# A hybrid decoder layer in split precision: low parts and square sums one step behind, four operand buffers in the down stages, and square sums by matmul

## Chip, core and metric

The kernel runs on one core of a Trainium2 chip. The metric is the device time of one execution in microseconds (us); the median of three executions is compared. TensorE (PE in the views) multiplies, VectorE (DVE) and ScalarE (ACT) do the element work, GpSimd (POOL) a little of it, and SyncE (SP) and GpSimd issue the DMAs.

## What is computed

One decoder layer on 1024 tokens of width 1024, in float32: a gated feed-forward network, a mixing block (windowed attention beside an mLSTM, their gated sum through an output matrix), a second network, and a final norm.

```
x = x + 1/2 * SwiGLU_1(RMSNorm(x))
h = RMSNorm(x); z = h @ W_in + b_in
...
x = x + (sigmoid(g_attn) * y_attn + sigmoid(g_mlstm) * y_mlstm) @ W_out
x = x + 1/2 * SwiGLU_2(RMSNorm(x))
final: RMSNorm(x).
...
def rms_norm(x, g):
    xf = x.astype(jnp.float32)
    y = xf * lax.rsqrt(jnp.mean(xf * xf, axis=-1, keepdims=True) + NORM_EPS)
    return (y * g.astype(jnp.float32)).astype(x.dtype)

def swiglu(x, w_gate, w_up, w_down):
    return (jax.nn.silu(x @ w_gate) * (x @ w_up)) @ w_down
```

## The kernel before

**Two parts of a number.** A float32 operand is split into a high part that TensorE takes (ScalarE copies and rounds it) and a low part, the difference (DVE subtracts). A product is three matmuls: high by high, high by low, low by high. The function `parted` issues copy and subtraction one behind the other, so that the subtraction is next on DVE when the copy has just gone to ScalarE. Weights (buffers `whi`, `wlo`, four of each) and activations are split in this way.

**Seven products instead of eight.** In both networks the operands are cut in halves in both directions, and seven products of sums replace eight. They have numbers; `PRODUCTS` gives the order 1, 2, 6, 7, 5, 4, 3. The tokens are cut into two halves of 512, h = 0 and 1. Sums of the weights' quarters are made on DVE by `sum_of`.

**The first stage of a network (`gate_up`)** goes through 11 steps s, in each through seven products p, for each of gate and up (w), with 12 matmuls of 128 x 512 each (L421); a few steps at the beginning take the products in a different order, since the activations for products 6, 7, 5, 4 and 3 come from the generator `lead`, which the code advances between the products. Weights are split by `split` ahead of their use, and the evacuations (L429 to L469) end in the combination of the seven products. Its results are written to a buffer `gd` in HBM.

**The second stage (`ffn`)**, called the down stage here, walks over three chunks c of the inner dimension (4, 4 and 3 tiles: `DOWN`) and seven products p; a step (c, p) takes its moving operand from `gd` with one DMA (`fetch`, L571, 2 MB or 1.5 MB, issued by GpSimd) into one of two buffers, and does four groups dp of 12 or 9 matmuls times the chunk's tiles (L632). The chunk's weights (`load`, from `dn`, four DMAs on SyncE) go to two buffers by turns. In the last chunk the outputs are complete and `done` is called for each of them: it takes their squares for the next norm.

**Norms.** `stats` squares one 128 x 512 tile on ScalarE (L253) and adds it to a running sum on DVE (L255). `rstd_rows` sums over partitions by four small matmuls (L262), adds the epsilon on DVE and takes the power on GpSimd (L264). `spread` brings the result to all partitions by four transposes (L270) and a copy on ScalarE (L272).

**The order** is written by hand: within a function by the order of the calls, across stages by generators. `pump()` advances those in the list `bg` (norm of the next stage, constants) by one yield each; `prepare()` issues the next weight's split. All engines run their own instructions in the order in which they are issued, and wait for each other by semaphores.

**Seams between stages**, by their place in the profile: the start (0 to 34 us), first network's first stage (to 458 us) and down stage (to 680 us), mixing of the two halves (L316 to L318 are its large products; the boundary of the halves is at 1205 us), the output product of the second half (L1481 adds the residual, L1449 is the first multiplication of the second network's norm for the first half), second network's first stage (from 1770 us) and down stage (from 2225 us), and the final norm at the end.

## Time and profile before

| what | value |
| --- | --- |
| median of 3 runs | 2463.17 us (2459.67 to 2466.4) |
| profiled execution, its own time | 2461.28 us |
| span in the profile | 2459.5 us |
| TensorE busy | 2357.0 us (96% of the span) |
| DVE busy | 1741.3 us (71%) |
| ScalarE busy | 940.8 us (38%) |
| GpSimd busy | 259.6 us (11%) |
| mean granted clock of TensorE | 0.980 |

The profiled execution lasts 1.8 us longer than its span, which begins with the first instruction. The granted clock is 1.00 at full speed and 0.50 at half; a mean over a stretch between them says how much of it ran at half. Busy time of TensorE contains matmuls that run slower at half clock, so 96% does not mean that only 4% is lost.

### The profile page before, as it was taken

What the parts mean: (1) busy time and instruction counts of PE and PEld (TensorE: products, weight loads), DVE (VectorE), ACT (ScalarE), POOL (GpSimd) and SP (SyncE); (2) the same over time, 40 slices, a digit from 0 to 9 for tenths busy, and PEclk for the clock granted to TensorE, in tenths of its full rate; (3) what the DMA queues carried; (4) which work ended last, traced back from release to release, by engine and by line L of the source; (5) the groups of instructions that cost most, each with busy time, mean ns of one, the idle gap of its engine ahead of it and who ended that gap; (6) DMA issues with size and microseconds to landing.
All of it is one profiled execution on the core that took longest, in us unless ns stands there. A gap on an engine that the chain in (4) does not pass through costs nothing.

```text
span 2459.5 us, 30117 instructions
## 1 busy us (share of the span) xinstructions
PE 2357.0 (96%) x11094; PEld 1951.4 (79%) x11094; DVE 1741.3 (71%) x2780; ACT 940.8 (38%) x1664; POOL 259.6 (11%) x246
## 2 busy tenths in 40 slices
PE   8899999989988999999999999999999999999995
PEld 7788888778877878888777878888778888887885
DVE  6989888856768864555568854545579987887666
ACT  5334334312236642333346632333343433332223
POOL 0000000000045320000134410000000000000001
PEclk8999999999999999999999999999999999999997
DMA  5355443995621213222541222222535544569653
GB/s 187 103 192 179 156 154 129 345 343 176 226 90 61 67 61 99 69 83 83 161 123 48 61 71 88 80 80 86 191 117 168 191 156 146 169 232 364 228 191 126
DMA packets 154324, 361.46 MB, mean 147 GB/s; under 512 B 13504, under 2 KB 22848, under 8 KB 154176
## 3 DMA queue, kind: packets, MB, share of 16 engines
q1 hardware_dynamic: 131728, 277.79, 34.5%
q0 software_dynamic: 21584, 81.53, 9.8%
q8 instruction: 88, 1.44, 0.2%
q14 instruction: 60, 0.49, 0.1%
q10 hardware_dynamic: 864, 0.21, 0.0%
HBM read 263.27 MB, written 96.21 MB: 146 GB/s over the span
## 4 chain that ended last, share of the span: by engine, by line
PE 58%; DVE 16%; issue 16%; DMA 5%; ACT 3%; POOL 1%; SPq 0%; DVEq 0%; POOLq 0%; ACTq 0%
PE mm L421 15%; PE mm L632 11%; PE mm L316 8%; PE mm L318 7%; PE mm L317 7%; DMA s<-gd 3%; DVE P L1048 1%; PE mm L909 1%; DVE PT L1087 1%; PE mm L910 1%; PE mm L911 1%; DMA gd<-nsq 1%; DVE wlo L336 1%; DVE P L1068 1%; DVE wlo L87 1%
## 5 line engine op out<-in xcount | busy, mean ns | idle before, releaser
L421 PE MATMUL mm<-s,whi 128*128 128x512 f32 x2112 | 657.4, 392 | 13.5 <-ACT nsq L460 8.7
L421 PEld LDWEIGHTS mm<-s,whi 128*128 128x128 f32 x2112 | 399.3, 189 | 99.9 <-ACT nsq L460 9.5
L316 PE MATMUL mm<-s,whi 128*128 128x512 f32 x1056 | 424.4, 402 | 1.0 <-ACT whi L75 1.0
L318 PE MATMUL mm<-s,wlo 128*128 128x512 f32 x1056 | 416.6, 394 | 6.2 <-DVE wlo L87 4.7
L317 PE MATMUL mm<-s,whi 128*128 128x512 f32 x1056 | 414.9, 393 | 0.0
L421 PE MATMUL mm<-s,wlo 128*128 128x512 f32 x1056 | 413.7, 392 | 0.0
L632 PE MATMUL mm<-s,whi 128*128 128x512 f32 (+1 forms) x1256 | 388.2, 391 | 14.0 <-DMA s<-gd 12.8
L632 PEld LDWEIGHTS mm<-s,whi 128*128 128x128 f32 x1256 | 237.7, 192 | 65.0 <-issue 10.3
L632 PE MATMUL mm<-s,wlo 128*128 128x512 f32 (+1 forms) x628 | 244.7, 390 | 0.0
L318 PEld LDWEIGHTS mm<-s,wlo 128*128 128x128 f32 x1056 | 200.2, 190 | 52.5 <-DVE wlo L87 6.0
L316 PEld LDWEIGHTS mm<-s,whi 128*128 128x128 f32 x1056 | 200.7, 190 | 42.7 <-issue 2.8
L421 PEld LDWEIGHTS mm<-s,wlo 128*128 128x128 f32 x1056 | 200.0, 189 | 41.6
L317 PEld LDWEIGHTS mm<-s,whi 128*128 128x128 f32 x1056 | 200.8, 190 | 38.1
L87 DVE TENSOR_TENSOR wlo<-wraw,whi 128x1024 fp32r<-128x1024 f32 (+1 forms) x138 | 169.6, 1229 | 67.2 <-ACT whi L75 66.6
L75 ACT ACTIVATE whi<-wraw 128x1024 fp32r<-128x1024 f32 (+1 forms) x154 | 159.7, 1042 | 68.1 <-DMA wraw<-wpa 20.6
L335 ACT ACTIVATE whi<-wr 128x1024 fp32r<-128x1024 f32 (+1 forms) x122 | 127.8, 1048 | 129.7 <-PE mm L421 83.3
L336 DVE TENSOR_TENSOR wlo<-wr,whi 128x1024 fp32r<-128x1024 f32 (+1 forms) x122 | 147.8, 1212 | 36.6 <-ACT whi L335 36.6
L335 ACT ACTIVATE whi<-s 128x1024 fp32r<-128x1024 f32 (+1 forms) x72 | 71.1, 987 | 250.9 <-PE mm L632 239.0
L571 POOL DMA_DIRECT2D s<-gd x42 | 31.8, 756 | 1165.6 <-PE mm L421 404.8
L632 PEld LDWEIGHTS mm<-s,wlo 128*128 128x128 f32 x628 | 120.2, 191 | 24.2
L336 DVE TENSOR_TENSOR nsq<-nsq 128x512 fp32r<-128x512 f32 x162 | 110.4, 685 | 24.4 <-ACT nsq L335 23.9
L429 ACT ACTIVATE nsq<-nsq 128x512 f32<-128x512 f32 x66 | 41.8, 633 | 216.6 <-DVE nsq L469 205.2
(274 smaller groups left out, 3519.5 us busy)
## 6 DMA issues: line engine op xcount, KB each, us to landing
gd<-nsq SPq DMA_DIRECT2D x308, 256.0 KB, 3.1
s<-gd POOLq DMA_DIRECT2D x28, 2048.0 KB, 10.6
wraw<-win SPq DMA_DIRECT2D x84, 512.0 KB, 3.6
wr<-gu SPq DMA_DIRECT2D x74, 512.0 KB, 4.7
s<-gd POOLq DMA_DIRECT2D x14, 1536.0 KB, 6.7
s<-dn SPq DMA_DIRECT2D x16, 1024.0 KB, 12.4
wraw<-gu SPq DMA_DIRECT2D x30, 512.0 KB, 4.8
nsq<-x SPq DMA_DIRECT2D x32, 256.0 KB, 6.8
```

Source lines behind the costliest of these rows:

```text
L75: self.nc.scalar.activation(hv, v, AF.Copy)
L87: (self.nc.gpsimd if self.on_pool else self.nc.vector).tensor_sub(lv, v, hv.bitcast(F32))
L316: nc.tensor.matmul(ps, hi, xh, start=first, stop=False)
L317: nc.tensor.matmul(ps, hi, xl, start=False, stop=False)
L318: nc.tensor.matmul(ps, lo, xh, start=False, stop=last)
L335: nc.scalar.activation(hi, x, AF.Copy)
L336: nc.vector.tensor_sub(lo, x, hi.bitcast(F32))
L421: nc.tensor.matmul(ps, a[:, k], op[p](k, x), start=first and k == 0 and j == 0, stop=k == 3 and j == 2, skip_group_check=not first)
L429: nc.scalar.activation(t, z[0], AF.Tanh, scale=0.5)
L571: nc.gpsimd.dma_start(t, gd[PRODUCTS.index(p), s0:s0 + a].rearrange("s p i t -> p s i t"))
L632: nc.tensor.matmul(ps, wt[:, f], t[:, f, x, c], start=first and f == 0 and q == 0, stop=f == a - 1 and q == 2, skip_group_check=not first)
L909: nc.tensor.matmul(ps, x[:, 0], hi, start=k == 0, stop=False)
```

## The change

- `parted` no longer issues the subtraction: it returns a function, and the caller calls it later. In the weights' splits (`gate_up`, `ffn`) the high part is issued in the first half of a product's work and the low part in the second, just ahead of the sums and loads that stood there; in the operands of a norm (`mixed`, `early`) and in the products' combination (L460 to L469) the low part comes one tile behind its high part.
- `stats` holds its addition back until the next square has been issued; `flush` issues what is left ahead of the sum over partitions.
- In the start, the second half's squares are no longer added up on DVE: `mean_square` sums each over partitions on TensorE, all eight into one PSUM tile. 16 matmuls on an identity matrix (`warm`) follow, and only then the first product.
- The down stages take the products in the order 1, 2, 6, 7, 4, 5, 3. They have four buffers for the moving operand, and a fetch is issued three steps ahead. The weights of all chunks share one place of four quarters, and the next chunk's quarters are loaded as soon as their place has been read.
- Two small ones: the tile `nv` of a norm has two buffers, and at the boundary of the halves the norm waits for eight pumps instead of three.

```diff
+DOWN_ORDER = (1, 2, 6, 7, 4, 5, 3)
...
     def stats(pool, acc, x, first, eng=nc.vector):
+
         sq = pool.tile([128, HS], F32, name="nsq", bufs=nbufs(pool))[:, :x.shape[-1]]
         nc.scalar.activation(acc if first else sq, x, AF.Square)
+        flush()
         if not first:
-            eng.tensor_add(acc, acc, sq)
...
+            held.append(lambda: eng.tensor_add(acc, acc, sq))
...
+    def mean_square(ps, sq, k):
+
+        for b in range(4):
+            nc.tensor.matmul(ps[:, b], sq[:, 128 * b:128 * b + 128], mean, start=k == 0 and b == 0,
+                             stop=k == KT - 1 and b == 3, skip_group_check=True)
...
     def parted(x, hi, lo):
         nc.scalar.activation(hi, x, AF.Copy)
-        nc.vector.tensor_sub(lo, x, hi.bitcast(F32))
+        return lambda: nc.vector.tensor_sub(lo, x, hi.bitcast(F32))
...
                 part = [temp(pool, R32) for _ in range(2)]
-                parted(x, *part)
+                lo = parted(x, *part)
+                yield
+                lo()
                 for i in range(2):
                     nc.sync.dma_start(gd[PRODUCTS.index(p), s, :, i], part[i].bitcast(F32))
-                yield
                 if sub:
                     sub[0](*sub[1:])
-                    yield
...
-            split(*nxt)
+            lo = split(*nxt)
+            yield
+            lo()
             done += 1
...
-        steps = [(c, p) for c in range(len(DOWN)) for p in PRODUCTS]
+        steps = [(c, p) for c in range(len(DOWN)) for p in DOWN_ORDER]
...
-            if b == 0:
-                raw[c] = slot((0, 2, 0)[c], [16 * HS], F32)
-            m, h = divmod(b, 2)
-            t = raw[c][:, b * 4 * a * 128:][:, :4 * a * 128]
+            if c == m == h == 0:
+                raw["all"] = slot(0, [4, 4 * HS], F32)
+            place = {(0, 0): 0, (0, 1): 3 if c == 1 else 1, (1, 0): 2, (1, 1): 1 if c == 1 else 3}[m, h]
+            t = raw["all"][:, place, :4 * a * 128]
...
-                t = moving["buf"][:, i % 2, :a]
+                b = (i + 1) % 4
+                t = moving["buf", b // 2][:, b % 2, :a]
...
+            yield
+            low()
+            if p in (1, 2, 6, 7):
+                sum_of(c, j, {1: 3, 2: 2, 6: 1, 7: 4}[p])
+            if j and c + 1 < len(DOWN) and p in (7, 4, 5, 3):
+                load(c + 1, *{7: (0, 0), 4: (0, 1), 5: (1, 0), 3: (1, 1)}[p])
+            yield
...
             elif p == 7:
-                moving["buf"] = slot(1, [2, 4, 2, HS])
+                moving["buf", 0] = slot(1, [2, 4, 2, HS])
                 fetch(0)
-                fetch(1)
...
+            elif p == 4:
+                moving["buf", 1] = slot(2, [2, 4, 2, HS])
+                for i in range(1, 4):
+                    fetch(i)
...
             if i:
-                fetch(i + 1)
+                fetch(i + 3)
...
-            if 1 <= i % 7 <= 4 and c < last:
-                load(c + 1, i % 7 - 1)
...
+        ps1 = psum.tile([128, 4, 2], F32, name="mm")
+
+        def square1(k):
+            sq = temp(pool)
+            nc.scalar.activation(sq, X[k][1], AF.Square)
+            mean_square(ps1, sq, k)
+
+        for k in range(5):
+            square1(k)
         for r in rs:
             pass
+        for k in range(5, KT):
+            square1(k)
+        warm(16)
...
-        bg.append(norm(op, psum, lambda k: xb[:, k], 1, Hcur))
+        bg.append(norm(op, psum, lambda k: xb[:, k], 1, Hcur, wait=8))
...
         for k in range(KT):
             nc.vector.scalar_tensor_tensor(X[k][0], X[k][0], gains[:, 2, k:k + 1], r, op0=OP.mult, op1=OP.mult)
-            parted(X[k][0], t0[:, k, 0], t0[:, k, 1])
-            yield
+            nxt = parted(X[k][0], t0[:, k, 0], t0[:, k, 1])
+            if lo:
+                lo()
+            lo = nxt
```

How this moves instructions is seen in the programs' order at three places. Line numbers are each kernel's own. First TensorE at the start, of the kernel before: matmuls on the identity, the first half's mean sums (L262), their spread (L270) and the first product (L421).

```order
L691 MATMUL mm<-ident 128x128 x36
L262 MATMUL mm<-mean,nsq 128x2 x4
L270 MATMUL mm<-ident,nv 128x128 x4
L421 MATMUL mm<-s_135,whi 128x512 x2
L421 MATMUL mm<-s_135,wlo 128x512
```

The same place after the change: L273 and L281 are the sums and the spread of the first half, L289 the second half's sums, L735 the warming matmuls, L443 the first product.

```order
L718 MATMUL mm<-ident 128x128 x36
L273 MATMUL mm<-mean,nsq 128x2 x4
L289 MATMUL mm<-mean,nsq 128x2 x20
L281 MATMUL mm<-ident,nv 128x128 x4
L289 MATMUL mm<-mean,nsq 128x2 x12
L735 MATMUL mm<-ident 128x128 x16
L443 MATMUL mm<-s_135,whi 128x512 x2
L443 MATMUL mm<-s_135,wlo 128x512
```

Five of the eight sets of sums have come ahead of the spread, three sets and 16 matmuls between it and the first product.

Second, DVE during the output product before the second network, before the change: L87 is a low part of the weights, L1481 the residual, L1449 the multiplication of the norm and L336 the low part of its result, L255 the addition of a square.

```order
L87 TENSOR_TENSOR wlo<-wraw,whi 128x1024
L1481 SCALAR_TENSOR_TENSOR nsq<-mm,nsq 128x512
L1449 SCALAR_TENSOR_TENSOR nsq<-nsq,gains 128x512
L336 TENSOR_TENSOR s_13653<-nsq,s_13653 128x512
L1449 SCALAR_TENSOR_TENSOR nsq<-nsq,gains 128x512
L336 TENSOR_TENSOR s_13653<-nsq,s_13653 128x512
L87 TENSOR_TENSOR wlo<-wraw,whi 128x1024
L1449 SCALAR_TENSOR_TENSOR nsq<-nsq,gains 128x512
L336 TENSOR_TENSOR s_13653<-nsq,s_13653 128x512
L1481 SCALAR_TENSOR_TENSOR nsq<-mm,nsq 128x512
L255 TENSOR_TENSOR nsq<-nsq 128x512
```

And after it (L88, L1529, L1491, L353 and L264 in that order):

```order
L1529 SCALAR_TENSOR_TENSOR nsq<-mm,nsq 128x512
L1491 SCALAR_TENSOR_TENSOR nsq<-nsq,gains 128x512 x2
L353 TENSOR_TENSOR s_13689<-nsq,s_13689 128x512
L88 TENSOR_TENSOR wlo<-wraw,whi 128x1024
L1529 SCALAR_TENSOR_TENSOR nsq<-mm,nsq 128x512
L1491 SCALAR_TENSOR_TENSOR nsq<-nsq,gains 128x512
L353 TENSOR_TENSOR s_13689<-nsq,s_13689 128x512
L1491 SCALAR_TENSOR_TENSOR nsq<-nsq,gains 128x512
L353 TENSOR_TENSOR s_13689<-nsq,s_13689 128x512
L88 TENSOR_TENSOR wlo<-wraw,whi 128x1024
L1529 SCALAR_TENSOR_TENSOR nsq<-mm,nsq 128x512
L264 TENSOR_TENSOR nsq<-nsq 128x512
```

The low part L353 of a tile now stands behind the multiplication L1491 of the next tile, instead of directly behind its own.

Third, DVE close to the end, before the change, with the buffers' numbers: L674 and L675 add a product to an output, L255 adds a square to the sum, L336 is a low part of the weights. The sum nsq_18662 belongs to the second half of the tokens, nsq_18486, which follows, to the first.

```order
L336 TENSOR_TENSOR wlo_18693<-s0_18006,whi_18692 128x768
L674 TENSOR_TENSOR nsq_17726<-nsq_17726,nsq_18456 128x512
L675 TENSOR_TENSOR nsq_17726<-mm_18682,nsq_17726 128x512
L255 TENSOR_TENSOR nsq_18662<-nsq_18662,nsq_18698 128x512
L674 TENSOR_TENSOR nsq_17728<-nsq_17728,nsq_18469 128x512
L675 TENSOR_TENSOR nsq_17728<-mm_18702,nsq_17728 128x512
L255 TENSOR_TENSOR nsq_18662<-nsq_18662,nsq_18714 128x512
L336 TENSOR_TENSOR wlo_18730<-s0_18006,whi_18729 128x768
L674 TENSOR_TENSOR nsq_17644<-nsq_17644,nsq_18426 128x512
L675 TENSOR_TENSOR nsq_17644<-mm_18719,nsq_17644 128x512
L255 TENSOR_TENSOR nsq_18486<-nsq_18486,nsq_18735 128x512
```

After the change (L701, L702, L264 and L353):

```order
L701 TENSOR_TENSOR nsq_17759<-nsq_17759,nsq_18462 128x512
L702 TENSOR_TENSOR nsq_17759<-mm_18749,nsq_17759 128x512
L264 TENSOR_TENSOR nsq_18522<-nsq_18522,nsq_18746 128x512
L353 TENSOR_TENSOR wlo_18760<-s0_17199,whi_18759 128x768
L701 TENSOR_TENSOR nsq_17761<-nsq_17761,nsq_18477 128x512
L702 TENSOR_TENSOR nsq_17761<-mm_18769,nsq_17761 128x512
L264 TENSOR_TENSOR nsq_18764<-nsq_18764,nsq_18782 128x512
L274 TENSOR_SCALAR nv_18785<-mm_18787 128x4
L701 TENSOR_TENSOR nsq_17763<-nsq_17763,nsq_18492 128x512
L702 TENSOR_TENSOR nsq_17763<-mm_18794,nsq_17763 128x512
L701 TENSOR_TENSOR nsq_17765<-nsq_17765,nsq_18506 128x512
```

Before, an addition L255 adds the square of the output that the row above has just completed; now L264 adds the square of the output one before, and the sum nsq_18522, which belongs to the first half, ends while the second half's begins (nsq_18764).

## Rows read from the trace of the kernel before

**Rows 1.** Page, part 1: busy us, share of the span, instructions.
```profile
PE 2357.0 (96%) x11094; PEld 1951.4 (79%) x11094; DVE 1741.3 (71%) x2780; ACT 940.8 (38%) x1664; POOL 259.6 (11%) x246
```

**Rows 2.** TensorE's waits, whole span: total us, times, longest us.
```profile
PE mm L632 <- DMA s<-gd: 12.8, 6, 3.4
PE mm L262 <- DVE nsq L255: 9.1, 2, 7.7
...
PE mm L421 <- ACT nsq L460: 8.7, 2, 4.7
PE mm L270 <- POOL nv L264: 8.6, 3, 5.1
...
PE mm L318 <- DVE wlo L87: 4.7, 3, 2.2
...
PE mm L421 <- DVE nsq L469: 4.3, 4, 2.3
PE mm L884 <- POOL s L308: 4.3, 5, 1.4
```

**Rows 3.** Windows by stage: busy us per engine (instructions), clock, DMA share, GB/s.
```profile
200.00:440.00 240.00, 240.00 (x1061) 198.72 (x1060) 200.64 (x261) 93.19 (x129) 0.00 (x0) 1.00 0.48 158
60.00:160.00 100.00, 92.31 (x391) 75.17 (x390) 94.07 (x139) 37.81 (x56) 0.35 (x1) 0.97 0.40 133
470.00:560.00 90.00, 81.42 (x343) 66.09 (x342) 54.68 (x67) 20.40 (x24) 5.38 (x8) 0.96 0.91 326
668.00:708.00 40.00, 32.18 (x165) 27.01 (x164) 27.10 (x37) 11.83 (x19) 16.51 (x15) 0.87 0.40 135
1185.00:1237.00 52.00, 47.44 (x204) 39.08 (x203) 32.42 (x38) 21.17 (x32) 12.89 (x9) 0.93 0.55 175
1743.00:1781.00 38.00, 32.24 (x125) 25.15 (x124) 24.99 (x32) 13.38 (x19) 0.00 (x0) 0.91 0.52 164
...
2225.00:2275.00 50.00, 44.83 (x195) 35.85 (x194) 32.86 (x42) 10.03 (x11) 2.97 (x4) 1.00 1.07 388
...
2420.00:2446.00 26.00, 13.08 (x74) 12.79 (x74) 16.57 (x34) 9.50 (x20) 1.73 (x2) 0.69 0.21 81
```

**Rows 4.** Timeline of the start: start us, us, engine, line, operation.
```profile
1.50 10.74 PE L691 MATMUL mm<-ident 128*128 128x128 f32 x72 [1.50 <-DVE ident L165]
...
12.08 0.95 PE L262 MATMUL mm<-mean,nsq 128*128 128x2 f32 x8
...
13.29 2.31 ACT L253 ACTIVATE nsq<-nsq 128x512 f32<-128x512 f32 x4
...
15.31 0.65 PE L270 MATMUL mm<-ident,nv 128*128 128x128 f32 x4 [2.27 <-POOL nv L264]
...
19.09 1.52 PE L421 MATMUL mm<-s,whi 128*128 128x512 f32 x2 [3.13 <-ACT s L727]
```

**Rows 5.** Window of the first products, columns as in rows 3.
```profile
19.00:30.50 11.50, 9.70 (x20) 6.26 (x21) 9.75 (x17) 5.38 (x10) 0.00 (x0) 0.50 0.37 144
```

**Rows 6.** TensorE's waits between 470 and 560 us.
```profile
PE mm L632 <- DMA s<-gd: 8.6, 3, 3.4
```

**Rows 7.** Timeline: a fetch, and the matmul that reads it.
```profile
469.44 0.74 POOL L571 DMA_DIRECT2D s<-gd  x1 [25.47 <-PE mm L632]
...
482.44 0.73 PE L632 MATMUL mm<-s,whi 128*128 128x512 f32 x2 [2.42 <-DMA s<-gd]
```

**Rows 8.** Page, part 6: KB each, us to landing.
```profile
s<-gd POOLq DMA_DIRECT2D x28, 2048.0 KB, 10.6
```

**Rows 9.** Timeline at the ends of the first down stage and of mixing's first half.
```profile
687.47 13.09 POOL L308 TENSOR_TENSOR s<-nsq,s 128x512 fp32r<-128x512 f32 x8 [5.96 <-ACT s L306]
...
1205.78 1.86 PE L262 MATMUL mm<-mean,nacc 128*128 128x2 f32 x8 [4.56 <-DVE nacc L255]
```

**Rows 10.** DVE's waits between 1739 and 1766 us.
```profile
DVE s L336 <- ACT s L335: 5.6, 8, 0.7
```

**Rows 11.** DVE's waits between 2402 and 2448 us.
```profile
DVE nsq L255 <- ACT nsq L253: 8.3, 14, 0.8
```

More of the change, by code (lines that the diff above doesn't have):

```diff
@@ L248, in drain, with flush @@
             pump()
+    held = []
+    def flush():
+        while held:
+            held.pop()()
     def stats(pool, acc, x, first, eng=nc.vector):
@@ L363, in mixed @@
         yield 7
-        for p, m, h in ((5, 0, 1), (4, 4, 0)):
+        rest = None
+        for p, m, h in ((5, 0, 1), (4, 4, 0), (3, 4, 1)):
             for k in range(4):
-                parted(X[m + k][h], op[p](k, 0), op[p](k, 1))
-                if k % 2:
-                    yield p if k == 3 else None
-        for k in range(4):
-            own[k] = [temp(pool, R32) for _ in range(2)]
-            parted(X[4 + k][1], *own[k])
-            if k % 2:
-                yield 3 if k == 3 else None
+                if p == 3:
+                    own[k] = [temp(pool, R32) for _ in range(2)]
+                nxt = parted(X[m + k][h], op[p](k, 0), op[p](k, 1))
+                if rest:
+                    rest()
+                rest = nxt
+                if k == 0 and p != 5:
+                    yield {4: 5, 3: 4}[p]
+                elif k % 2:
+                    yield
+        rest()
+        yield 3
     def gate_up(n, pool, psum, op, gd, lead, tail, ahead):
@@ L501, in gate_up @@
         rest = iter(order)
-        for _ in range(2):
-            split(*next(rest))
+        for lo in [split(*next(rest)) for _ in range(2)]:
+            lo()
         yield
@@ L510, in prepare @@
             if nxt is None:
-                ahead()
+                yield from ahead()
                 return
-            split(*nxt)
+            lo = split(*nxt)
+            yield
+            lo()
             done += 1
@@ L524, in prepare @@
                 sum_of(0, 3), sum_of(0, 2)
-            return nxt
-        for _ in range(2):
-            prepare()
+            behind(*nxt)
+            yield
+        for g in [prepare() for _ in range(2)]:
+            next(g), next(g)
         ready = {1, 2}
@@ L532, in gate_up @@
                 ready.add(next(lead))
-            nxt = None
+            step = prepare() if j else None
             for w in range(2):
                 for _ in group(s, p, w):
-                    if w == 0 and j:
-                        nxt = prepare()
-                    elif nxt:
-                        behind(*nxt)
+                    if step:
+                        next(step, None)
                 for _ in range(2 - w):
@@ L656, in ffn @@
                     ps = times(i, moving[i], dp, cols)
-                    if dp % 2 == 0 and span[0] != QUARTERS[1][0]:
-                        t = prepare()
-                    elif dp % 2 and t:
-                        sum_of(*t)
-                        t = None
+                    if dp % 2 == 0:
+                        step = prepare() if span[0] != QUARTERS[1][0] else None
+                    if step:
+                        next(step, None)
                     add = nc.vector.tensor_add
@@ L699, in lead @@
         def lead():
-            for _ in range(4):
-                yield
-            for r in rstd_of(pool, psum, acc[1:]):
+            for r in rs1:
                 yield
@@ L705, in lead, with warm @@
             bg.append(late_consts(pool))
+        def warm(n):
+            ps = psum.tile([128, HS], F32, name="mm")
+            for b in range(n):
+                nc.tensor.matmul(ps[:, 128 * (b % 4):128 * (b % 4) + 128], ident, ident, start=True, stop=True)
         for k in range(KT):
@@ L730, in layer @@
                 nc.vector.tensor_sub(o(j % 4, 1), X[j][0], o(j % 4, 0).bitcast(F32))
-            if k % 2 and k < KT:
-                stats(pool, acc[1], X[4 + k // 2][1], False)
+            if k == 4:
+                next(rs1)
         Hm = []
```

52 lines of the change are left out of this document (28 added, 24 removed).

## The prediction

> **What bounds the kernel now.** I read the page first, then TensorE's chain of waits, then windows by stage, and timelines where a wait stood. TensorE is busy for 2357.0 of 2459.5 us [rows 1], so at most about 100 us of idle time are to be had, and beside them what TensorE loses where its clock is halved (1.2 instead of 2.4 GHz). In the steady first product stage (gate and up, 200 to 440 us) there is nothing to win: 1061 matmuls in 240 us, 0.2262 us each, clock 1.00, TensorE never idle, VectorE (DVE) busy for 200.64 [rows 3]. The losses stand at the seams between stages. The list of waits says on whom: fetches of the down stage's operand 12.8 us, the norm's sums 9.1, broadcasts of the norm (the chain over GpSimd) 8.6, ScalarE and DVE evacuations of the products 8.7 and 4.3, the weights' low parts 4.7, the first half's norm inputs 4.3 and 3.1 [rows 2]. The reader should see that none of these is long; each is also followed by a stretch at half clock. What that costs I take from the clock column: a stretch of 40 us with a mean clock of 0.87 lost 40 x 0.13 = 5.2 us of TensorE's pace [rows 3]. It is an upper bound, since part of it may be idle time.
>
> The profiled execution takes 2461.28 us as a whole, 1.9 below the median 2463.17 of the runs; the sum is made against 2461.28.
>
> **The change, part by part.**
>
> *Start (lines 697 to 732).* Removed: the second half's seven accumulations on DVE, of which four stood among the first products' operands. Added on TensorE ahead of the first product: eight sets of mean matmuls and 16 warming matmuls (32 records). A set takes 0.95 us now; a warming record at most 10.74 / 72 = 0.15, so 4.8 for all [rows 4]. ScalarE makes the squares at 2.31 / 4 = 0.58 each from 13.3, the fifth is done at 16.2, its set at 17.1, the spread at 17.8; the copy of it and three more squares end at about 20, the eighth set at 21.1, the warming at 25.9. So the first product starts at 25.9 instead of 19.09 [rows 4]. In the kernel before, though, the eleven us after 19 held only 20 matmuls at clock 0.50 [rows 5]; done without gaps at full clock, 20 take 4.5 us and end at the same 30.5. If the clock stays up, the start itself is even. If it halves at about 17 us (it was at half from 19 on before [rows 5]), sets take twice as long (1.86, the value of the set at 1205.78 [rows 9]): two of the five first sets, the spread, three more sets and the warming end at about 34, and 20 matmuls are done at 38.6, 8 us later than before. Against this stands what the earlier second norm and lighter DVE remove further on: between 60 and 160 us TensorE is idle for 100 - 92.31 = 7.7 us (4.0, the 8.7 less the longest, for an evacuation on ScalarE, the rest for those on DVE, which is busy for 94.07) and loses 100 x 0.03 = 3.0 of clock [rows 2, 3]; 10.7 together. The stretch up to the first product has only small work in both kernels, so half clock is likelier (60%): **3** us, between -3 (half clock, and half of the stalls stay) and 11.
>
> *First down stage (L571, L632).* Now a fetch goes into one of two buffers, and can be issued only when the step before has released its buffer: issued at 469.44, used at 482.44, after a wait of 2.42 [rows 7]. One step is 48 matmuls x 0.2262 = 10.9 us, and the fetch took 13.0; 10.6 is the median [rows 8]. With four buffers a fetch is issued three steps ahead, 32 us, which covers it. Waits of 8.6 us in three places [rows 6] and 90 x 0.04 = 3.6 of clock [rows 3] go: 12.2. I take **11**, since the first fetches still meet the loads of the second chunk; bounds 2 and 12.2. The Trainium skill's page "DMA: Bandwidth & Descriptors" (section "Where 436 GB/s comes from") says that traffic between HBM and SBUF is limited to some 358 GB/s per core; by that the 90 us x 326 GB/s = 29.3 MB of this stretch need 82 us and the term would be 8, the sum 3 worse. The trace does not agree: it moved 388 GB/s between 2225 and 2275 us [rows 3].
>
> *Down stages to what follows: first one to mix (668 to 708).* With product 4 moved ahead of 5 the first half of the tokens is complete one step (36 matmuls, 8.1 us) earlier, and its norm is emitted earlier. TensorE is idle for 40 - 32.18 = 7.8 us there, 4.3 of it for low parts on GpSimd [rows 2, 3], and loses 5.2 of clock: 13. The eight low parts on GpSimd last 13.09 us, 1.64 each [rows 9], while the matmuls that use one take less; this chain stays as it is, only started earlier. **7.5**, between 4 and 11.
>
> *First half to second half (1205).* TensorE waits 4.56 for the accumulation and then runs at half clock [rows 9]; 52 x 0.07 = 3.6 of clock [rows 3]. The norm is now emitted five pumps later, which gives DVE some 6.8 us (five times about six matmuls x 0.2262): **7** of 8.2, down to 4 if DVE's queue is later still.
>
> *Output product to second FFN (1743 to 1781).* DVE waits 5.6 us in eight places for the high part just ahead of each low part [rows 10]; the lag takes the low part behind the next multiplication. TensorE's idle time there, 38 - 32.24 = 5.8 us with 4.7 for the weights' low parts, follows from it, and 38 x 0.09 = 3.4 of clock [rows 2, 3]: 9.2, of which **8.5**; at least 5.
>
> *Second lead (1825).* The 4.7 us wait for an evacuation on ScalarE [rows 2] is of the same kind: DVE was held by low parts. With its clock **5.5**, 3 to 7.
>
> *Second down stage.* 12.8 - 8.6 = 4.2 of fetch waits [rows 2, 6]; **4**, 1 to 6.
>
> *Tail (2402 to the end).* DVE waits 8.3 us in 14 places for the square just issued [rows 11]; TensorE waits 7.7 and 5.1 for DVE and GpSimd [rows 2] at a mean clock of 0.69 [rows 3]. With one square's lag the 8.3 go, and product 4 gives the first half's norm a step more. From the sum on DVE: **10**, bounds 6 (TensorE becomes the limit) and 14.
>
> Sum: 3 + 11 + 7.5 + 7 + 8.5 + 5.5 + 4 + 10 = 56.5. Seams that are removed usually leave a smaller wait behind: the load of the next chunk is now issued just ahead of the DVE sum that reads it, and waits for its landing. I take off 4.5 for such waits at eight seams, and predict 2461.28 - 52 = **2409 us**; a median may stand to it as that of before does, up to 2 us higher.
>
> What is costed at nothing: the lag itself in the steady stages. A product's low part now stands in its second half on DVE instead of its first. What hides it is the lead of the weights' buffers (four, products three ahead) and DVE's 16% of free time [rows 3].
>
> **The rivals.**
>
> *The low part comes too late (slower).* In the steady stage a low part now comes half a product later, 12 matmuls x 0.2262 = 2.7 us. If the lead of three products were used up by other work ahead of it on DVE, each of 154 products in two FFNs would wait. It decides from 0.34 us a product on (52 / 154); at 0.4 the time is 2409 + 62 = 2471. Against it: DVE is 84% busy and TensorE waits for nothing for 240 us [rows 3]. 3%.
>
> *Transfers bind in the down stages.* More buffers only move the wait from issue to landing, if the DMA engines are full: 0.91 of them between 470 and 560 us, 1.07 between 2225 and 2275 [rows 3]. Then 11 + 4 are lost: 2424. Against it: a fetch of 2 MB in 10.6 us [rows 8] is 198 GB/s, little over half of the 388 GB/s that the busiest stretch moved, and the full state is short. 13%.
>
> *The clock stays full at the start.* The sets and the warming keep TensorE occupied: 8 us better, 2401. For it: matmuls without gaps from 13 to 26 us. Against it: the first matmuls at 12.08 and 15.31 [rows 4], of the same small kind, did not hold it. 17%.
>
> *DVE's work, not its waits, is the limit at the seams.* Then the lag shifts a wait from ScalarE to nothing gained: half of the terms of lead, output product, mix and tail (7.5 + 8.5 + 5.5 + 10 = 31.5, so 16) and the 5 of the start's stalls come back: 2430. For it: DVE is busy for 27.10 of 40 and 24.99 of 38 us [rows 3], not more, which speaks against; yet the start's DVE was nearly full. 15%.
>
> *Nothing but shifted waits.* The gains at one seam are lost at the next: 2455 to 2467. 5%.
>
> **How the numbers follow.** The forecast has 44% (its own range is 2398 to 2420), the rivals 3, 13, 17, 15 and 5, and 3 are left for better than all. The range 2388 to 2438 takes in all but the first and last rival and the worse part of the fourth. About 0.3% (7 us) is what a measurement of this kernel can tell from no change. Faster by over that: 0.92; within: 0.04 (most of the last rival); slower: 0.04 (the first, and a little of the last).
>
> **What would show it.** Right: no wait for fetches between 470 and 560 and between 2225 and 2275 us; TensorE's waits at 67, 1205, 1754 and 1825 us below 1 us each; DVE's waits for squares in the tail near 0; the first product near 34 us, and the clock at 0.5 from about 17 us. Wrong: waits of TensorE for low parts in the steady stage; fetches that land later than 30 us after their issue; a first product at 34 us with the stalls at 67 and 101 us still there; a DVE busy without gaps at the seams.

## The result and the profile after

The changed kernel takes 2428.33 us (median of four runs, 2426.23 to 2430.49), against 2462.1 for the kernel before on the same chip: a ratio of 0.9861, 95% interval [0.9844, 0.9878], 33.8 us faster. On another chip it measured 2425.03 against 2463.42, 0.9847 [0.9832, 0.9862]. The forecast was 2409, with a range of 2388 to 2438: the direction was right, the gain 65 to 74% of the one forecast. The profiled execution took 2426.23 us, with a span of 2424.5.

The line that answers to [rows 1] shows hardly less work on TensorE; what changed is the span around it:

```profile
PE 2356.4 (97%) x11182; PEld 1958.6 (81%) x11182; DVE 1727.2 (71%) x2773; ACT 944.9 (39%) x1664; POOL 261.9 (11%) x246
```

TensorE's waits, as in [rows 2], total us, times, longest:

```profile
PE mm L273 <- DVE nsq L264: 9.7, 5, 3.6
...
PE mm L443 <- DVE nsq L491: 4.9, 5, 1.4
PE mm L273 <- DVE nacc L264: 3.9, 1, 3.9
PE mm L281 <- POOL nv L275: 3.2, 2, 2.0
PE mm L662 <- issue: 2.8, 1, 2.8
...
PE mm L926 <- DVE wlo L88: 2.2, 2, 1.4
```

The waits for fetches and for evacuations on ScalarE are gone, and those for the weights' low parts on DVE are down from 4.7 to 2.2 us. One wait of 2.8 us in the first down stage is new; for it the profile shows no releaser ("issue"). The waits for the norm's sums (L273, 9.7 and 3.9 us), which had been 9.1 and 4.56 [rows 2, 9] and were to go too, have stayed. The windows of [rows 3], moved with their stages (busy us of PE, PEld, DVE, ACT and POOL, then the clock, the DMA share and GB/s):

```profile
200.00:440.00 240.00, 240.00 (x1060) 198.74 (x1059) 196.25 (x255) 93.39 (x126) 0.96 (x1) 1.00 0.48 159
60.00:160.00 100.00, 97.84 (x429) 80.09 (x428) 91.27 (x135) 39.67 (x58) 0.35 (x1) 1.00 0.46 152
467.00:557.00 90.00, 86.84 (x383) 71.30 (x382) 62.30 (x76) 21.04 (x24) 5.42 (x8) 1.00 0.93 336
648.00:688.00 40.00, 33.99 (x152) 28.48 (x151) 29.62 (x39) 12.59 (x19) 15.87 (x15) 0.85 0.29 104
1175.00:1227.00 52.00, 47.34 (x209) 39.00 (x207) 30.51 (x36) 20.79 (x31) 13.25 (x9) 0.93 0.55 175
1723.00:1761.00 38.00, 38.00 (x170) 31.43 (x169) 25.68 (x35) 15.80 (x22) 0.00 (x0) 1.00 0.71 230
2203.00:2253.00 50.00, 49.47 (x219) 40.64 (x217) 32.42 (x43) 10.79 (x11) 2.96 (x4) 1.00 1.10 400
2385.00:2411.00 26.00, 19.36 (x112) 17.01 (x110) 18.27 (x37) 12.92 (x25) 2.10 (x2) 0.87 0.21 82
```

The reader should compare TensorE's busy time and the clock column. The down stages' entries (467 and 2203 us) and the output product (1723) are nearly full and at full clock; mixing's entry (648) and the half boundary (1175) are as bad as before. The steady stage is unchanged, 1060 matmuls in 240 us.

Because both programs do the same matmuls, the start of the same matmul in the two traces says how much has been gained up to there. By seams:

| from, to (matmul that marks the end; before, after) | forecast | measured | second trace |
| --- | --- | --- | --- |
| start and first product stage (first L632: 458.10, 455.15) | 3 | 2.95 | -1.16 |
| first down stage, up to its last chunk (623.09, 611.17) | 11 | 8.97 | 12.67 |
| to mixing's first full products (702.60, 689.58) | 7.5 | 1.10 | 4.25 |
| mixing and the half boundary (1240.68, 1230.92) | 7 | -3.26 | -4.31 |
| second half, output product, norm (1787.45, 1769.24) | 8.5 | 8.45 | 8.94 |
| second product stage with its lead (2209.29, 2187.03) | 5.5 | 4.05 | -0.37 |
| second down stage, up to its last chunk (2367.95, 2340.73) | 4 | 4.96 | 6.08 |
| tail (spans 2459.5, 2424.5) | 10 | 7.78 | 8.32 |

The last column is read from the trace of the second measurement, at the same matmuls. The sums are 35.0 and 34.4; the forecast took 4.5 off its sum of 56.5. In the first trace two seams make up nearly all of the difference: the way to mixing (6.4 us short) and the half boundary (10.3 short). The last column says how far one execution stands for the kernel: single seams differ by up to 4.4 us between two executions of the same program. The half boundary is short by over 10 us in both; the way to mixing is 6.4 short in one and 3.3 in the other.

At the start, the timeline of the changed kernel:

```profile
21.53 5.28 PE L289 MATMUL mm<-mean,nsq 128*128 128x2 f32 x24 [1.21 <-ACT nsq L753]
...
26.67 5.81 PE L735 MATMUL mm<-ident 128*128 128x128 f32 x32
...
32.24 0.71 PE L443 MATMUL mm<-s,whi 128*128 128x512 f32 x2
```

The sums and the warming ran at half clock, and the first product came at 32.24 us, 13.2 later than before [rows 4]; the forecast had 34 for this case.

Why mixing did not gain is in the timeline of the changed kernel's last chunk in the first down stage. The last square of the first half's norm is ready on ScalarE at 655.19. Its addition (L264) is the last row of DVE here, behind an addition to an output and a low part of the weights and two more additions that are left out:

```profile
654.56 0.63 ACT L261 ACTIVATE nsq<-nsq 128x512 f32<-128x512 f32 x1 [2.29 <-DVE nsq L702]
...
655.77 0.69 DVE L702 TENSOR_TENSOR nsq<-mm,nsq 128x512 f32<-128x512 f32 x1
...
656.37 0.95 DVE L353 TENSOR_TENSOR wlo<-s,whi 128x768 fp32r<-128x768 f32 x1
...
658.64 0.68 DVE L264 TENSOR_TENSOR nsq<-nsq 128x512 f32<-128x512 f32 x1
...
659.37 1.87 PE L273 MATMUL mm<-mean,nsq 128*128 128x2 f32 x8 [3.16 <-DVE nsq L264]
```

The addition waits 3.5 us in a queue that it need not stand in, TensorE waits 3.16 for it, and its clock is at half from 658.9 to 665.7. The half boundary repeats it: the last square ends at 1190.21, its addition starts at 1197.91, behind two residual additions (L1446) with what belongs to them, and low parts of the weights:

```profile
1189.59 0.62 ACT L261 ACTIVATE nsq<-m 128x512 f32<-128x512 f32 x1
...
1192.33 0.68 DVE L1446 SCALAR_TENSOR_TENSOR xr<-mm,xr 128x512 f32<-128x512 f32 x1
...
1197.91 0.68 DVE L264 TENSOR_TENSOR nacc<-nacc,nsq 128x512 f32<-128x512 f32 x1
...
1198.65 1.86 PE L273 MATMUL mm<-mean,nacc 128*128 128x2 f32 x8 [3.90 <-DVE nacc L264]
```

`stats` issues an addition when the next square comes. For the last square there is no next one, so `rstd_rows` issues it, immediately ahead of the matmuls that read the sum. The longer wait of the norm at the boundary moved the matmuls later, and the last addition with them.

### The profile page after: what moved, and what is told of

The parts are those of the page before. It is cut to its first block, busy times and chain, and to the rows that moved or that the text cites. A ratio compares the mean times of both kernels' runs of the same rounds, so it can differ in the third digit from the quotient of the medians.

```text
span 2424.5 us, 30289 instructions
## 1 busy us (share of the span) xinstructions
PE 2356.4 (97%) x11182; PEld 1958.6 (81%) x11182; DVE 1727.2 (71%) x2773; ACT 944.9 (39%) x1664; POOL 261.9 (11%) x246
## 4 chain that ended last, share of the span: by engine, by line
PE 73%; DVE 17%; DMA 3%; ACT 3%; issue 3%; SPq 0%; POOL 0%; DVEq 0%; ACTq 0%
PE mm L443 26%; PE mm L662 15%; PE mm L333 8%; PE mm L334 7%; PE mm L335 7%; DVE wlo L353 2%; DMA gd<-nsq 2%; DVE P L1089 2%; PE mm L950 1%; DVE PT L1128 1%; PE mm L951 1%; PE mm L952 1%; DVE wlo L88 1%; DMA wr<-gu 1%; DVE P L1109 1%
## 5 line engine op out<-in xcount | busy, mean ns | idle before, releaser
L443 PE MATMUL mm<-s,whi 128*128 128x512 f32 x2112 | 650.8, 389 | 0.0
L443 PEld LDWEIGHTS mm<-s,whi 128*128 128x128 f32 x2112 | 396.1, 188 | 82.1
L443 PE MATMUL mm<-s,wlo 128*128 128x512 f32 x1056 | 410.8, 389 | 0.0
L443 PEld LDWEIGHTS mm<-s,wlo 128*128 128x128 f32 x1056 | 198.2, 188 | 41.1
L88 DVE TENSOR_TENSOR wlo<-wraw,whi 128x1024 fp32r<-128x1024 f32 (+1 forms) x138 | 170.6, 1237 | 68.4 <-ACT whi L76 67.9
L352 ACT ACTIVATE nsq<-nsq 128x512 fp32r<-128x512 f32 x162 | 98.8, 624 | 140.6 <-DVE nsq L353 59.9
L353 DVE TENSOR_TENSOR wlo<-wr,whi 128x1024 fp32r<-128x1024 f32 (+1 forms) x122 | 147.5, 1209 | 8.1 <-ACT whi L352 8.0
L491 DVE TENSOR_TENSOR nsq<-mm,nsq 128x512 f32<-128x512 f32 x132 | 90.4, 685 | 58.0 <-PE mm L443 57.9
## 6 DMA issues: line engine op xcount, KB each, us to landing
s<-gd POOLq DMA_DIRECT2D x28, 2048.0 KB, 13.5
```

Of the source, the lines that this page charges most:

```text
L88: (self.nc.gpsimd if self.on_pool else self.nc.vector).tensor_sub(lv, v, hv.bitcast(F32))
L352: nc.scalar.activation(hi, x, AF.Copy)
L353: return lambda: nc.vector.tensor_sub(lo, x, hi.bitcast(F32))
L443: nc.tensor.matmul(ps, a[:, k], op[p](k, x), start=first and k == 0 and j == 0, stop=k == 3 and j == 2, skip_group_check=not first)
L491: nc.vector.tensor_add(st[s, to, w], ps, st[s, key, w])
```

## The experiments

They ran on three chips, four kernels on each in the order of the table, and the kernel before beside them (2458.70, 2459.36 and 2463.42 us). Ratios are against it, with a 95% interval. Times of different chips are compared by the ratios: 0.001 is 2.46 us. All experiments are edits of the changed kernel. Each trace is of one of a kernel's four executions, which are up to 8.5 us apart; those of two buffers, of no hold and of the old start are of the slowest of the four, those of the old loads and of the weights' low parts at once of the fastest.

| kernel | us | ratio |
| --- | --- | --- |
| early issue of the last additions | 2418.52 | 0.9831 [0.9813, 0.9849] |
| norm waits three pumps | 2427.25 | 0.9864 [0.9843, 0.9886] |
| both | 2417.19 | 0.9827 [0.9807, 0.9847] |
| two buffers | 2431.92 | 0.9888 [0.9868, 0.9908] |
| no hold of the additions | 2425.98 | 0.9864 [0.9849, 0.9880] |
| two buffers, old loads | 2442.89 | 0.9926 [0.9912, 0.9941] |
| weights' low parts at once | 2440.02 | 0.9922 [0.9905, 0.9938] |
| old start | 2428.84 | 0.9875 [0.9859, 0.9891] |
| the changed kernel again | 2425.03 | 0.9847 [0.9832, 0.9862] |
| no warming | 2429.52 | 0.9866 [0.9851, 0.9882] |
| early issue, later spread | 2412.64 | 0.9792 [0.9776, 0.9809] |
| early issue, earlier reload | 2415.97 | 0.9807 [0.9791, 0.9823] |

**Early issue of the last additions.**

```diff
-        for _ in range(wait):
+        for i in range(wait):
             yield
+            if i == 0:
+                flush()
```

and the same in the final norm and the second network's lead.

> The changed kernel, with the last held addition of a norm's square sum issued one pump after its square instead of just ahead of the sum over partitions (in the norms ahead of mixing, the final norm and the second network's lead). Theory: the holding back of that last addition is what makes TensorE wait at 659 us (3.16 us) and at 1199 us (3.90 us), each with a stretch at half clock behind it (6.8 us, so 3.4 lost). Then both waits fall below 1 us and the time is 2428 - 12 = about 2416 (2412 to 2420). Rival: DVE is simply behind with real work at these places, or the later start of the norm at the half boundary is to blame: then the waits stay above 2.5 us and the time is within 3 us of 2428.

2418.52 us. Its timeline at the way to mixing:

```profile
654.70 0.63 ACT L261 ACTIVATE nsq<-nsq 128x512 f32<-128x512 f32 x1 [2.29 <-DVE nsq L704]
...
655.36 0.69 DVE L264 TENSOR_TENSOR nsq<-nsq 128x512 f32<-128x512 f32 x1 [0.16 <-ACT nsq L261]
...
656.18 0.98 PE L273 MATMUL mm<-mean,nsq 128*128 128x2 f32 x8
...
659.63 0.15 DVE L274 TENSOR_SCALAR nv<-mm 128x4 f32<-128x4 f32 x1
...
659.94 1.65 POOL L275 TENSOR_TENSOR nv<-nv,mhalf 128x4 f32<-128x4 f32 x1 [22.93 <-DVE nv L274]
...
661.64 0.65 PE L281 MATMUL mm<-ident,nv 128*128 128x128 f32 x4 [2.27 <-POOL nv L275]
```

The last addition now follows its square, the sums (L273) start without a wait, and 3.16 us are gone at this place; the 3.90 at the boundary too. The theory holds, the rival of a DVE behind with real work does not. By the ratios the time is 4 or 7 us below the two measurements of the changed kernel, with intervals that overlap; two further kernels that contain this edit are 9.1 and 12.4 us below the changed kernel on one chip, with intervals clear of it (the last two experiments). A smaller wait has come in its place: the epsilon (L274) starts 2.5 us after the sums have ended, since DVE's queue stands ahead of it, the power on GpSimd takes 1.65, and the spread (L281) waits 2.27 for it.

**Three pumps at the boundary.**

```diff
-        bg.append(norm(op, psum, lambda k: xb[:, k], 1, Hcur, wait=8))
+        bg.append(norm(op, psum, lambda k: xb[:, k], 1, Hcur, wait=3))
```

> The changed kernel with the norm at the boundary of the halves waiting three pumps again instead of eight. If the longer wait alone put DVE's work (two residual additions, their squares and low parts) between the last square and its addition, the wait of 3.90 us at 1199 comes back at its place of before with about 4 to 5 us, and the time is within 2 us of 2428: the held addition is issued late with either wait. If the later start of the norm is itself what costs the 10 us that the boundary lost against the forecast, the time falls by 5 us or more, to 2423 or less.

```profile
PE mm L273 <- DVE nacc L264: 7.7, 1, 7.7
```

2427.25 us. The wait at the boundary rose to 7.7 us, more than expected, and yet the time did not change: the norm is earlier, and waits behind it (1.45 us at 1229 in the changed kernel) are gone. So the eight pumps neither brought nor cost anything that can be measured.

**Both together**, by the two diffs above.

> The early issue of the last additions and three pumps at the boundary of the halves together. If with the addition issued early eight pumps only delay the norm, this one is faster than the early issue with eight pumps, by up to 3 us. If three pumps are too few for the sum to be ready, as in the kernel before, TensorE waits 3 to 5 us at the boundary again, and it is 4 to 7 us slower than the early issue with eight pumps.

2417.19 us, within 1.4 of the early issue alone on the same chip, in spite of a wait of 5.65 us at the boundary. The wait of the second expectation came, its 4 to 7 us did not; a gain of 1.3 can't be told from none. A wait there costs about as much as the delay that avoids it.

**Two buffers.**

```diff
-                t = moving["buf", b // 2][:, b % 2, :a]
+                t = moving["buf", 0][:, i % 2, :a]
...
-                fetch(i + 3)
+                fetch(i + 1)
```

and two fetches in the first product stage instead of four.

> The changed kernel with two buffers for the moving operand again and fetches one step ahead, all else as changed. The forecast's account (11 us in the first down stage and 4 in the second, of which the comparison of the two traces shows 9 and 5) says 2428 + 14 = 2442 (2438 to 2446), with the waits of TensorE for fetches back. Rival: the fetch waits went because of the new places of the weights' loads and their times, not because of the buffers; then the time is within 4 us of 2428.

```profile
PE mm L658 <- DMA s<-gd: 5.9, 5, 1.5
```

2431.92 us, 3.6 slower than the first measurement of the changed kernel, where 14 were expected; by the ratios, 7 to 10 slower. Waits for fetches come back, but 5.9 us instead of 12.8, and none long enough for a stretch at half clock. By the same matmuls the two down stages lose 0.8 and 2.3 us against the first trace, 4.5 and 3.4 against the trace of the second measurement, which did not have the wait of 2.8 us at 523 us.

**Two buffers and the old loads.**

```diff
-            if j and c + 1 < len(DOWN) and p in (7, 4, 5, 3):
-                load(c + 1, *{7: (0, 0), 4: (0, 1), 5: (1, 0), 3: (1, 1)}[p])
...
+            if 1 <= i % 7 <= 4 and c < last:
+                load(c + 1, *divmod(i % 7 - 1, 2))
```

and two places for the weights instead of one.

> The kernel with two buffers again, and beside it the down stage's weights loaded as before: two places by turns, a chunk's four loads issued at its first steps instead of behind the splits. Two buffers alone cost only 3.6 us of the 14 that the two down stages gained. If the new times of the weights' loads are the rest, this one is at 2432 + 9 = 2441 (2437 to 2446) and fetches wait in the first chunk for 8 us or more as before. If they are not, and the rest came from the product order, the time stays at 2432 within 3.

```profile
PE mm L655 <- DMA s<-gd: 9.7, 7, 2.8
```

2442.89 us, 11 slower than two buffers alone (9 by the ratios), as the theory had it, though the waits in the first down stage are 5.7 us and not 8. Its trace shows 5.0 and 3.5 us of loss in the down stages, against 0.8 and 2.3, so 5.3 of the 11 are seen there. The new places and times of the loads are worth about as much as the buffers; what the old ones cost beside four buffers was not run. In the kernel before eight loads of the next two chunks, 7 MB, were issued between 471 and 525 us beside the fetches; the changed one issued four, 4 MB, between 490 and 525, since each waits until its place has been read.

**No hold.**

```diff
-        flush()
         if not first:
-            held.append(lambda: eng.tensor_add(acc, acc, sq))
+            eng.tensor_add(acc, acc, sq)
```

> The changed kernel with the square sums not held back: each addition directly behind its square, as before; all other lags stay. If the hold is what costs at mixing and at the half boundary, the waits at 659 and 1199 us fall as with the early issue (10 us gained there), and what the hold gives in the last stage comes back as DVE's waits for squares (8.3 us in 14 places before; the last stage gained 8 in all). The forecast's pricing of the tail (10 us, mostly by the hold) says 2418.5 + 8 = 2426. If the product 4 that comes a step earlier made the tail's gain, and not the hold, the time stays near that of the early issue, 2416 to 2421.

DVE's waits in the tail, which are 1.1 us in the changed kernel:

```profile
DVE nsq L263 <- ACT nsq L261: 6.2, 11, 0.8
```

2425.98 us: the hold as it was made is worth nothing in all, since its gain in the tail is paid at the other norms. By the same matmuls this kernel loses 7.4 us in the tail against the first trace and gains 3.9 at the half boundary and 1.7 on the way to mixing. So the hold made the tail's gain; without it product 4, which still comes a step earlier, leaves 0.4 of the 7.8.

**Weights' low parts at once.**

```diff
-            lo = split(*nxt)
-            yield
-            lo()
+            split(*nxt)()
+            yield
```

and the same in `ffn`.

> The changed kernel with the weights' low parts again directly behind their high parts (in both stages of the networks); the lags in the norms' operands, in the combination of products and in the square sums stay. Forecast's account: in the steady stages the lag is worth nothing (TensorE never waits there), and the leads at 67 and 1825 us gained partly by it: 2428 + 3 to 7, about 2433. Rival: the low parts' lag only moves work within DVE's queue, and nothing changes: 2425 to 2431. Third: the lag delays the evacuations at 126 and 1858 us (new waits of 1 to 2 us each), and taking it away gains 3: 2425.

TensorE's waits in the second lead:

```profile
PE mm L443 <- ACT nsq L482: 4.5, 1, 4.5
```

2440.02 us, 12 to 15 slower (15 to 18 by the ratios): all three expectations were too small. The wait of the kernel before at 1825 us (4.7) is back almost to the digit, and by the same matmuls 5.4 us are lost at 65 to 71 us and 6.2 at 1802 to 1806 us, against either trace of the changed kernel. No other single edit costs as much (the two on the transfers together cost 16 to 19), and the leads are where the lag of the weights' low parts acts.

**The old start.** The second half's sums on DVE, no warming; the removed lines of the start's diff stand again.

```diff
-        for k in range(5):
-            square1(k)
+        for k in range(4):
+            stats(pool, acc[1], X[k][1], k == 0)
...
-        warm(16)
```

> The changed kernel with the start of before: the second half's squares are added up on DVE, no warming, the first product at about 19 us. The traces show that the new start is 13.2 us late at the first product and has made it good, by 4.7 us, at 105 us. If the sums on TensorE and the earlier second norm did that, the old start is slower, 2428 + 3 to 8, with TensorE's waits at 67 and 101 us back. If the lags alone did it, the old start keeps its 6 to 8 us and is at about 2421.

```profile
PE mm L443 <- DVE nsq L491: 5.8, 2, 4.7
```

This is the list of TensorE's waits between 10 and 160 us. 2428.84 us, between the two expectations; the ratio is 0.001 to 0.003 above those of the changed kernel's two measurements. In its trace it is 13.3 us ahead at the first product, 1.7 ahead at 98 us, 3.7 behind at 131 and 6.8 behind at 452, with 5.8 us of waits for DVE's evacuations (2.1 in the changed kernel). Of the 6.8, 3.3 came at once at 452 us, in a wait of 3.4 us at the end of the product stage, where the next run finds one in the changed kernel too; up to there it is 3.6 behind the first trace and 0.7 behind the second. So the new start pays its late beginning back, by what DVE no longer has to do; how much more, between 0 and 7 us, the runs do not settle.

**The changed kernel again.** No edit.

> The changed kernel itself, once more, on the chip of the three below, so that they can be compared with it directly: 0.986 of the kernel before, within 0.002.

2425.03 us, 0.9847. Its trace differs from the first one where it matters below: there is no wait at 523 us in the first down stage, the first product comes at 34.3 us, the half clock ahead of mixing lasts 3.4 us instead of 6.8, and TensorE waits for an evacuation on DVE (L491) at the end of both product stages, 1.3 us at 456 and 3.1 at 2184 of this trace. Of DVE ahead of the first of these:

```profile
452.66 0.69 DVE L353 TENSOR_TENSOR nsq<-nsq 128x512 fp32r<-128x512 f32 x1 [4.05 <-DMA gd<-nsq]
...
455.66 0.68 DVE L491 TENSOR_TENSOR nsq<-mm,nsq 128x512 f32<-128x512 f32 x1
```

The evacuation stands behind a low part that waits for a write of results to HBM (`gd`). The kernel before has no such wait of TensorE; of the thirteen traces of the changed kernel and its variants, twelve have one of 0.3 to 3.4 us at one end or both, most often over 1 us. These writes took 4.5 us in the median in the changed kernel and 3.1 in the one before (page, part 6). What lengthened them was not tried.

**No warming.**

```diff
-        warm(16)
```

> The changed kernel without the 16 warming matmuls. In the changed kernel's trace the warming ran at half clock and ended at 32.2 us, 1.3 us after the clock had come back at 30.9. Theory one: the warming only fills the time in which the clock comes back; without it the first product starts about 5.5 us earlier at half clock, does half as much there, and gains 2 to 3 us (2425). Theory two, the forecast's: its time is simply added, the first product comes 5.5 us earlier and the kernel gains 5 us (2423). Theory three: without it the clock stays at half until later, and the kernel loses 2 us or more.

```profile
16.00:28.00 12.00, 10.79 (x52) 10.39 (x52) 4.68 (x8) 4.88 (x9) 0.00 (x0) 0.51 0.63 243
28.00:33.00 5.00, 5.00 (x14) 4.03 (x14) 5.00 (x9) 2.39 (x5) 2.05 (x1) 0.50 0.00 0
```

2429.52 us, 4.5 slower than the changed kernel on the same chip, with intervals that overlap. The first product came at 28.34, but at half clock to 33.2 us; against the changed kernel's second trace it is 6 us ahead at first, 3 at 136 us, and 1.0 at the second down stage's first matmul. The time speaks for theory three, the trace for none; it stays open.

**Early issue and a later spread.** The early issue, and two more pumps between the sums and the spread:

```diff
         yield
         yield
+        for _ in range(more):
+            yield
         yield spread(pool, psum, v, n)
```

> The early issue of the last additions, and beside it two more pumps between the sum over partitions and the spread of a norm (ahead of mixing and in the final norm's first parts). With the early issue TensorE still waits at the spread for GpSimd's power: 2.27 us at 661, 1.70 at 1196 and 3.35 at 2380, the last two of three with half clock behind them. If the chain over DVE's queue and GpSimd is simply too long for two pumps, these waits fall below 1 us and the time is 8 to 10 us below that of the changed kernel of the early issue's 10, so 14 to 18 below it in all. If the later spread delays what comes behind (the operand of mixing, the final multiplications), the time is within 3 us of the early issue alone.

```profile
PE mm L928 <- ACT s L327: 3.9, 1, 3.9
PE mm L928 <- ACT whi L76: 3.2, 1, 3.2
PE mm L281 <- POOL nv L275: 2.4, 3, 1.3
```

2412.64 us, 12.4 below the changed kernel on its chip, the fastest of all. Waits at the spread fell from 8.9 to 2.4 us in all; two new ones, for mixing's first operands (L928, 3.9 and 3.2), stand at the entries of mixing's two halves: the spread now comes late for the first of them (ScalarE's copy of the norm's result, L327); the second is for a high part of the weights. It gained less than the 14 to 18 expected, but both effects were seen. How much the later spread adds to the early issue isn't shown: 10 us by the ratios, but only 3.3 against the next kernel, which holds the early issue on the same chip, with intervals that overlap. (In the early issue's trace half clock follows the spread's waits at 661 and 2380 us, not the one at 1196.)

**Early issue and an earlier reload.** The loads of the residual one step earlier in the down stage.

```diff
-            if i == 2:
+            if i == 1:
                 for d in range(0, KT, 2):
                     loadx(d, 1)
-            elif i in (3, 4):
+            elif i in (2, 3):
                 for d in range(1, KT, 2):
-                    loadx(d, i - 3)
+                    loadx(d, i - 2)
```

> The early issue of the last additions, and the reloads of the residual in the down stage issued one step earlier, since product 4 now needs them one step earlier. If TensorE's wait of 2.84 us at 523 us comes from the late reload (DVE waits for it until 521.8), it goes, with 2 to 4 us off the early issue's time. If the DMA engines are the limit there (share 1.1 between 455 and 530 us), the wait moves to the fetches or stays, and the time is the same within 2 us or longer.

2415.97 us, 9.1 below the changed kernel on the same chip. The wait at 523 us is absent, but it is also absent from the trace of the changed kernel's second measurement. So this run doesn't show that the reload caused it; what it does show, on the changed kernel's own chip, is the gain of the early issue.

## Why the prediction was right in direction and too large

**Right.** The output product (8.5; 8.45 and 8.94 in the two traces), the second down stage's gain (4; 4.96 and 6.08) and the steady stage, where the lag costs nothing, came out as forecast; no run takes the output product's lag out alone. The lead of the second network gained 7.3 us by 1866 us of the kernel before, 6.6 of it at its wait, and gave 3.15 back at two waits for evacuations on DVE (L491, 1.2 and 1.4 us).

**Right by luck** is the start's 2.95 for 3. The half clock was foreseen, and its two parts, -8 for the late start and 10.7 for the stalls behind it, were measured as -5.3 at 60 us and 8.7 by 162 us. But the second trace has -7.4 and 7.9, and -1.16 in all with the wait at the end of the product stage. And the forecast gave the 10.7 to the earlier second norm and a lighter DVE: 5.1 us of the 8.7 were gained at 65 to 71 us, where the old start loses nothing and the weights' low parts at once lose 5.4. That part belongs to the lag of the weights' low parts, which the forecast did not count there.

**The step that failed** is the one on the norms: "The norm is now emitted five pumps later, which gives DVE some 6.8 us" and "its norm is emitted earlier" (7 and 7.5 us). They take it that the sum is complete when DVE has done what was issued before the last square. With the held addition it is not: the addition is issued with the norm, whenever that is, and stands behind all that DVE got in between. The change has `flush` ahead of the sum over partitions for this, and the forecast gave it no price. The early issue shows the cause: both waits go, and 4 to 10 us with them, by the measurement of the changed kernel that one compares with; its trace is 10.2 us ahead of the first one. The two seams gain 5.2 and 2.6 us in it, for 7.5 and 7 forecast, so the held addition is 9.9 of the 16.7 us that they were short of in the first trace. A part of the rest is the norm's chain over DVE's queue and GpSimd, which then keeps TensorE waiting at the spread (2.27 and 1.70 us); the remainder stays open. With the later spread beside it the time is 2412.64, near the forecast's 2409.

**The small waits left behind**, for which the forecast took 4.5 off, were to be for loads issued late; DVE's waits for the down stages' loads are 1.1 us in all. They came at the ends of the product stages instead, in some executions.

**The mechanism that was half right** is the fetches: 9 and 5 us were gained (12.7 and 6.1 in the second trace) for 11 and 4 forecast, but not by the four buffers alone. The step "with four buffers a fetch is issued three steps ahead, 32 us, which covers it" is worth 3 to 10 us of the 14, by the trace or the ratio that one takes; the rest belongs to the loads' new places and times, which the forecast named only as a risk. The sentences on the 358 GB/s of the Trainium skill's page "DMA: Bandwidth & Descriptors" (section "Where 436 GB/s comes from") would have made the gain smaller; the trace moved 396 GB/s for 50 us (455 to 505) without a wait of TensorE.

**A size that was off** is the tail, 7.8 for 10 (8.3 in the second trace). DVE's 8.3 us of waits for squares fell to 1.1, as forecast. DVE's waits for TensorE grew from 4.2 to 6.8 us in a stretch of the same 46 us (6.3 of them in the 26 us shown below), and TensorE still waits 5.5 us for the norm's sums and 3.2 at the spread after 2340 us (8.4 and 6.3 before):

```profile
DVE nsq L702 <- PE mm L662: 6.3, 3, 3.7
DVE nsq L264 <- ACT nsq L261: 1.1, 2, 0.7
...
PE mm L273 <- DVE nsq L264: 5.5, 3, 3.6
```

The rival of DVE's work as the limit predicted 2430, close to the time, by luck. DVE was not full at the two seams; its order was wrong.

## What to carry to other kernels

When an engine's instruction is held back so that the next one's input can be made meanwhile, ask what issues the last one, and how much the engine has been given by then. When a transfer waits, look at what else is moved in the same stretch before adding buffers: here two buffers with the loads spread out lost 3 to 10 us, not 14. When a seam's gain in one trace agrees with a forecast, read a second trace of the same kernel before calling it right: here seams moved by up to 4.4 us. A low part taken out from directly behind its high part costs nothing where there is slack, and was worth 12 us or more at two leads where DVE's queue stood ahead of an evacuation.

## What was not expected of the hardware

A window of the changed kernel, with the columns as above:

```profile
16.00:32.00 16.00, 14.79 (x80) 14.39 (x80) 10.26 (x17) 7.55 (x14) 2.05 (x1) 0.57 0.46 177
```

TensorE was busy for 14.79 of these 16 us, and its mean clock there was 0.57: the sums over partitions (two columns each) and the spread did not hold the clock, which came back at 30.9, during the warming matmuls. Without these it came back at 33.2, five microseconds after the first product had begun.

A fetch of 2 MB took 13.5 us in the median instead of 10.6 [rows 8]; with two buffers and all else as in the changed kernel it took 8.4:

```profile
s<-gd POOLq DMA_DIRECT2D x28, 2048.0 KB, 13.5
...
s<-gd POOLq DMA_DIRECT2D x28, 2048.0 KB, 8.4
```

So fetches issued three steps ahead each took longer; the profile puts no wait of TensorE down to one of them.
